# Late sums of the down weights on VectorE, an addition moved up, and rows of x loaded one by one, in a one-core hybrid encoder layer

## The chip, the cores and the metric

The kernel runs on one core of one Trainium2 chip. The metric is the device time of that core in microseconds (us), from the first to the last instruction with what the launch adds around it; three runs are given and their median is the time. Five engines work in parallel, each through its own list of instructions in order: TensorE (PE; its weight loads are shown apart as PEld), VectorE (DVE), ScalarE (ACT), GpSimd (POOL) and SyncE (SP), which here does nothing but issue transfers. An instruction waits until the results that it needs have been signalled by other engines or by transfers. An engine whose next instruction waits does nothing else meanwhile.

## The reference

One layer of an encoder on 2048 prompt tokens and 64 sample tokens, all in float32. The first half is a pooled mixer and an mLSTM with an output projection; the second half, which this change touches, is a gated feed-forward network with a causal convolution of four taps over the tokens:

```python
h2 = rmsnorm(x, g2) * (1 + sc2) + sh2
up = h2 @ w_up
upp = jnp.concatenate([conv_buf.astype(up.dtype), up], 1)
conv = b_conv + sum(w_conv[j] * upp[:, j:j + T] for j in range(CONV_W))
a, g = jnp.split(conv, 2, -1)
x = x + gt2 * ((jax.nn.silu(g) * a) @ w_down)
...
y_prompt = rmsnorm(xp, g_final)
```

The outputs are y for both sequences and the states of the mixer, the mLSTM and the convolution.

## The kernel before, in words

All products of matrices are done in three passes over float32 numbers split into a high and a low part (high by high, high by low, low by high), so each weight tile that comes in (`raw`) is turned into a split tile (`wt`): ScalarE makes the high part (L385), VectorE the low part (L388).

The feed-forward network runs from about 805 us on, in three groups of 704 tokens (`fgroups`, group 0, 1, 2), each of two half-rows of 352. The 22 blocks of 128 inner channels are taken in parts: (0,5), (5,10), (10,16), (16,22) in groups 0 and 1, and (0,6), (6,10), (10,14), (14,18), (18,22) in group 2. In each part the up products of its blocks are made, and then the down product adds them to the sum for the eight rows of 128 output channels. A down product of group 2 also saves multiplications (`quad_down`, L1785 on): it takes quads of 2x2 weight blocks and needs, beside two of the blocks themselves, four sums of blocks, which are kept in device memory as `dsum`.

A block of the up product is a `Pair` (the a-half and the g-half of the gate). Its four products of half-rows are made from seven products of 12 matmuls each, in the manner of Strassen and Winograd, from sums of the inputs and sums of the weights: in order B11, B21, the old pair's T4, T2, T3, B22, T1 (L1570 on; the matmuls are those of L1547). Their results are put together on VectorE: `eg` and `ea` are the two channels' convolution inputs (L1555, and L1609 for half of `ea`, which is the result of B21 plus a copy of B11's), `ta` and `tg` the taps (L1535, with a scaling on ScalarE, L1530), then the silu on ScalarE (L1656), the gate (L1663, or L1703 where the result goes into quads), and the split of the gated rows into `av` (L1682 on ScalarE, L1692 on VectorE). `ea` reads the PSUM bank of B21; B22 writes into this bank next. The steps of two older pairs are woven into the products of the newest one.

Work of the stages that lie before or after is kept in six lists of generators (`bg[0]` to `bg[5]`); `tick(i)` runs list i one step further, up to its next `yield`. List 0 holds the final normalization of the group before (`final`: the updates of x at L1893 and the stores of y), list 1 the preparation of the next group (normalization, then `reload`, which fetches the next group's inputs), list 5 the sums of the down weights (`down_sums`, L1771). In the last part of group 2, `from_quads` (L1829) turns the Strassen sums back into rows and adds them to x: per couple of rows two additions (L1838, L1839) and four updates (L1843); x itself is loaded per row by `load_x2` (L1862).

The order on TensorE, VectorE, ScalarE and GpSimd is the order in which the program is written (`manual_schedule`); the transfers that SyncE issues are placed by a scheduler, except those that are marked to keep the order of the program. The weights come through SyncE's queue in the order of their use.

`down_sums` before: in 4 passes over column blocks, for each of the four sums, 4 transfers copy one summand to `dsum` through SyncE's queue (L1778), then 4 transfers issued by GpSimd (L1781) add the other summand on the way. Those are 64 copies and 64 adding transfers of 128 KB, spread over groups 0 and 1 (three ticks per pair).

## Time and profile before

| what | value |
|---|---|
| three runs | 2208.61, 2206.72, 2208.37 us; median 2208.37 |
| profiled execution | 2210.41 us, span 2208.6 us, granted clock 0.998 |
| TensorE, weight loads | busy 2176.4 us (99%), 2064.1 us (93%) |
| VectorE, ScalarE, GpSimd | 1626.1 us (74%), 1037.4 us (47%), 276.9 us (13%) |
| transfers | 521.68 MB, 236 GB/s on the mean |
| the feed-forward groups | about 804 to 1272, 1272 to 1740, 1740 to 2209 us |
| adding transfers of `dsum` (L1781) | 64 issues of 897 ns, from 825.9 to 1673.2 us |

A row of the groups reads: line, engine, operation, output <- input, shape, count, then busy time and mean ns of one, then the idle time of the engine just before the group and what ended it. A row of the timeline reads: start, length, engine, line, operation, names, count, and in brackets the idle time before it with its releaser. PEld rows show the weight loads that go ahead of each matmul. A row of the windows reads: the window, its length, the busy time of PE, PEld, DVE, ACT and POOL with their instructions, the granted clock, the share of the DMA engines and GB/s.

### The profile page before, as it was taken

How to read it: one execution, taken by the hardware profiler on the slowest of the kernel's cores; microseconds unless marked ns; L12 is line 12 of the kernel's file. 1: busy time of each engine (PE TensorE's matmuls, PEld its weight loads, DVE VectorE, ACT ScalarE, POOL GpSimd, SP SyncE). 2: the span in 40 equal slices, each digit the busy share in tenths (PEclk: the TensorE clock that was granted, in tenths of full speed). 3: DMA queues.
4: the chain of work that ended last, by engine and by line, in shares of the span. 5: the costliest groups of instructions: out<-in, count | busy, mean ns of one | idle time of the engine just before them, and what ended most of it. 6: DMA issues, size and time to landing. Idle time of an engine off the chain costs nothing. (4 is left out here: it accounts for less than half of the span.)

```text
span 2208.6 us, 38414 instructions
## 1 busy us (share of the span) xinstructions
PE 2176.4 (99%) x13708; PEld 2064.1 (93%) x13708; DVE 1626.1 (74%) x2996; ACT 1037.4 (47%) x2023; POOL 276.9 (13%) x546
## 2 busy tenths in 40 slices
PE   8999999999999999999999999999999999999998
PEld 7888888888899999999999999999999999999998
DVE  4887659577765768786958677776757597888894
ACT  3653335234243446464626444545435356554554
POOL 0010001001000101010202220101101321121122
PEclk9999999999999999999999999999999999999999
DMA  9978987997898687677858977767569665555552
GB/s 345 358 249 258 333 282 236 326 322 245 291 324 270 214 298 239 224 232 239 236 166 239 308 234 222 222 213 204 176 180 270 194 200 174 162 156 178 156 195 81
DMA packets 304192, 521.68 MB, mean 236 GB/s; under 512 B 27480, under 2 KB 131288, under 8 KB 304000
## 3 DMA queue, kind: packets, MB, share of 16 engines
q1 hardware_dynamic: 283008, 482.74, 66.8%
q10 hardware_dynamic: 11776, 28.09, 3.4%
q0 software_dynamic: 9216, 8.39, 3.1%
q8 instruction: 108, 1.77, 0.3%
q14 instruction: 84, 0.69, 0.1%
HBM read 408.36 MB, written 127.52 MB: 243 GB/s over the span
## 5 line engine op out<-in xcount | busy, mean ns | idle before, releaser
L1547 PE MATMUL mm<-hx,wt 128*128 128x352 f32 x5544 | 889.6, 321 | 10.0 <-DVE ea L1609 8.0
L1547 PEld LDWEIGHTS mm<-hx,wt 128*128 128x128 f32 x5544 | 879.5, 188 | 15.0 <-ACT wt L385 9.4
L442 PE MATMUL mm<-hl,wt 128*128 128x512 f32 (+2 forms) x1920 | 395.8, 358 | 1.4 <-DMA wt<-hl_kept 1.3
L2043 PE MATMUL mm<-av,wt 128*128 128x352 f32 (+2 forms) x2400 | 385.6, 321 | 1.6 <-ACT av L1682 0.9
L385 ACT ACTIVATE wt<-raw 128x512 fp32r<-128x512 f32 (+3 forms) x510 | 288.7, 579 | 205.5 <-PE mm L2043 64.6
L2043 PEld LDWEIGHTS mm<-av,wt 128*128 128x128 f32 x2400 | 380.7, 188 | 3.9 <-ACT av L1682 1.2
L388 DVE TENSOR_TENSOR wt<-raw,wt 128x512 fp32r<-128x512 f32 (+3 forms) x510 | 323.3, 648 | 73.6 <-ACT wt L385 71.3
L442 PEld LDWEIGHTS mm<-hl,wt 128*128 128x128 f32 x1920 | 312.7, 188 | 49.0 <-issue 2.8
L442 PE MATMUL mm<-mx,wt 128*128 128x512 f32 (+1 forms) x960 | 187.0, 354 | 0.3
L442 PEld LDWEIGHTS mm<-mx,wt 128*128 128x128 f32 x960 | 158.8, 188 | 25.8 <-ACT mx L1403 1.1
L385 ACT ACTIVATE wt<-wt 128x512 fp32r<-128x512 f32 x176 | 110.4, 628 | 123.8 <-DMA wt<-wsum 105.3
L388 DVE TENSOR_TENSOR wt<-wt 128x512 fp32r<-128x512 f32 x176 | 122.2, 694 | 58.9 <-ACT wt L385 58.5
L1535 DVE SCALAR_TENSOR_TENSOR tg<-eg,V,tg 128x704 f32<-128x704 f32 (+1 forms) x132 | 125.7, 952 | 40.9 <-ACT tg L1530 38.4
L2060 DVE SCALAR_TENSOR_TENSOR x<-mm,MOD,x 128x352 f32<-128x352 f32 (+4 forms) x152 | 78.0, 560 | 82.6 <-PE mm L2043 82.6
L1535 DVE SCALAR_TENSOR_TENSOR ta<-ea,V,ta 128x704 f32<-128x704 f32 (+1 forms) x132 | 125.7, 953 | 8.5 <-ACT ta L1530 5.9
L1796 PE MATMUL mm<-av,wt 128*128 128x352 f32 x576 | 94.4, 321 | 0.0
L1796 PEld LDWEIGHTS mm<-av,wt 128*128 128x128 f32 x576 | 91.8, 188 | 0.0
L207 DVE SCALAR_TENSOR_TENSOR acc<-raw,CA,acc 128x512 f32<-128x512 f32 x84 | 60.6, 748 | 30.8 <-DMA raw<-w_ada 30.7
L1656 ACT ACTIVATE tg<-tg 128x704 f32<-128x704 f32 (+1 forms) x66 | 52.3, 793 | 62.6 <-DVE tg L1535 62.6
L1555 DVE TENSOR_TENSOR eg<-mm,u 128x352 f32<-128x352 f32 x154 | 70.2, 468 | 14.8 <-ACT u L1625 10.1
L1605 ACT ACTIVATE u<-mm 128x352 f32<-128x352 f32 x66 | 30.3, 459 | 100.7 <-PE mm L1547 66.8
L1139 PE MATMUL mm<-wt,hl 128*128 128x256 f32 (+1 forms) x576 | 70.9, 282 | 0.0
(327 smaller groups left out, 2296.9 us busy)
## 6 DMA issues: line engine op xcount, KB each, us to landing
wt<-hl_kept SPq DMA_DIRECT2D x108, 512.0 KB, 5.9
raw<-w_up SPq DMA_DIRECT2D x198, 256.0 KB, 3.9
wt<-wsum SPq DMA_DIRECT2D x176, 256.0 KB, 4.8
wt<-wsplit SPq DMA_DIRECT2D x88, 512.0 KB, 4.8
w<-w_up SPq DMA_DIRECT2D x88, 256.0 KB, 5.4
wsum<-w SPq DMA_DIRECT2D x44, 512.0 KB, 6.2
wsplit<-wt SPq DMA_DIRECT2D x44, 512.0 KB, 4.4
raw<-w_down SPq DMA_DIRECT2D x88, 256.0 KB, 3.9
```

The costliest lines, as they stand in the source:

```text
L207: dve.scalar_tensor_tensor(out=acc[s], in0=w, scalar=CA[:, k, s:s + 1], in1=acc[s], op0=ALU.mult, op1=ALU.add)
L385: act.activation(u.w[:, 0, :u.n], u.raw[:, :u.n], AF.Copy)
L388: dve.tensor_tensor(out=u.w[:, 1, :u.n], in0=u.raw[:, :u.n], in1=u.w[:, 0, :u.n].bitcast(F32), op=ALU.subtract)
L442: pe.matmul(ps[bi][:, :hi - lo], U[:, a, k % 4 * P:(k % 4 + 1) * P], mv[k][:, b, lo:hi], start=(at == 0 and pi == 0), stop=(k == order[-1] ...
L1139: pe.matmul(ps[ti][:n, :cols], h[4 * kh + k4][:, b, lo:lo + n], U[:, a, k4 % 2 * cols:(k4 % 2 + 1) * cols], start=(kh == 0 and k4 == 0 and ...
L1535: dve.scalar_tensor_tensor(out=t[:, :E], in0=ext[:, j:j + E], scalar=wc(j, f), in1=t[:, :E], op0=ALU.mult, op1=ALU.add)
L1547: pe.matmul(ps[:, :FH], U[:, a, kc * P:(kc + 1) * P], Bo.at(nm, kc, b), start=(first and kc == 0 and pi == 0), stop=(kc == 3 and pi == 2), ...
L1555: dve.tensor_tensor(out=ext[:, d:d + b - a], in0=ps[:, a:b], in1=u[:, a:b], op=ALU.add)
L1656: act.activation(self.tg[:, :E], self.tg[:, :E], AF.Silu)
L1796: pe.matmul(ps, U[:, x, w:w + P], quad.d[nm][z], start=(start and k == 0 and pi == 0), stop=(k == 1 and pi == 2), skip_group_check=not start)
L2043: pe.matmul(ps[i][:, :hi - lo], U[:, a, k % 4 * P:(k % 4 + 1) * P], av[k](b, lo, hi), start=(k == 0 and (a, b) == PASSES[0]), stop=(k == n ...
L2060: dve.scalar_tensor_tensor(out=x3[n][:, a:b], in0=ps[i][:, a - lo:b - lo], scalar=gt2(n, s), in1=x3[n][:, a:b], op0=ALU.mult, op1=ALU.add)
```

## The change

1. `down_sums` is written anew. It enters list 5 at the third part of group 1 (part index 2) and first waits until list 1 is empty. Then it goes through 32 tiles: SyncE loads a tile of 2 KB per partition (one quad of blocks) from `w_quad`, which is laid out anew for this, into one of three tiles in rotation (`dq`, `rb`, `rbn`); VectorE makes the four sums in place by four additions of 128x128; GpSimd issues one store of the whole tile to `dsum`. List 5 is ticked once after each product (seven times per pair) and at every second step of a down product, and is emptied before group 2 begins. `dsum` has another layout, and `quad_units` and `quad_down` index it accordingly.
2. `ea` (now L1603) is added right after the taps of the old pair (L1534), ahead of `eg` and the weight split.
3. The rows of x in the first part of a group are loaded one at a time, each ahead of a row of the down product (`row(n)`), instead of all that are missing at once.
4. `final` of group 1 takes six ticks instead of three per row. `from_quads` has four steps per pair instead of six beside the last pairs, and what is left goes on list 1 in the last down product.
5. A small Silu on ScalarE is written ahead of the groups.

The order on TensorE is the same before and after but for names. Three places show what moves.

VectorE, a pair in the fourth part of group 1 (channels 16 to 21; `ta`, `tg` are the taps of the a- and the g-half, `wt<-wt` the low part of a summed weight, `wt<-raw,wt` that of a weight as loaded). Before:

```order
L388 TENSOR_TENSOR wt<-wt 128x512
L1535 SCALAR_TENSOR_TENSOR ta<-ea,V,ta 128x704 x2
L1555 TENSOR_TENSOR eg<-mm,u_18018 128x352
L388 TENSOR_TENSOR wt<-wt 128x512
L1609 TENSOR_TENSOR ea<-mm,s_18104 128x352
L1535 SCALAR_TENSOR_TENSOR tg<-eg,V,tg 128x704 x2
L388 TENSOR_TENSOR wt<-raw,wt 128x512 x2
```

Now:

```order
L1534 SCALAR_TENSOR_TENSOR ta<-ea,V,ta 128x704 x2
L1603 TENSOR_TENSOR ea<-mm,s_18089 128x352
L1555 TENSOR_TENSOR eg<-mm,u_17994 128x352
L387 TENSOR_TENSOR wt<-wt 128x512
L1786 TENSOR_TENSOR rb<-rb 128x128
L1787 TENSOR_TENSOR rb<-rb 128x128
L1788 TENSOR_TENSOR rb<-rb 128x128
L1789 TENSOR_TENSOR rb<-rb 128x128
L1534 SCALAR_TENSOR_TENSOR tg<-eg,V,tg 128x704 x2
L387 TENSOR_TENSOR wt<-raw,wt 128x512 x2
```

The addition of `ea` stands ahead of `eg` and of the weight split instead of behind them, and the four additions of a tile of the new sums stand between the split and the taps of the g-half. Such fours stand at three or four places of each pair of this part.

SyncE's queue in the same part (`wsum` and `wsplit` are sums of the up weights, `w_up` the weights themselves). Before:

```order
L369 DMA raw<-w_up 128x512 x3
L374 DMA wt<-wsplit 128x1024
L369 DMA raw<-w_up 128x512
L1778 DMA dsum<-dsum 128x256
L369 DMA raw<-w_up 128x512
L377 DMA wt<-wsum 128x512
L369 DMA raw<-w_up 128x512
L377 DMA wt<-wsum 128x512
L374 DMA wt<-wsplit 128x1024 x2
L377 DMA wt<-wsum 128x512
L1778 DMA dsum<-dsum 128x256
```

Now:

```order
L368 DMA raw<-w_up 128x512
L376 DMA wt<-wsum 128x512
L1780 DMA dq<-w_quad 128x512
L373 DMA wt<-wsplit 128x1024
L1780 DMA rbn<-w_quad 128x512
L373 DMA wt<-wsplit 128x1024
L1780 DMA rb<-w_quad 128x512
L376 DMA wt<-wsum 128x512
L1780 DMA rbn<-w_quad 128x512
L368 DMA raw<-w_up 128x512 x2
L376 DMA wt<-wsum 128x512
```

One copy in `dsum` every few rows has become a load of a whole tile about every second row, among the weights of the up products; each waits until the store of its tile's former content has landed.

SyncE's queue at the first down product of group 1. Before:

```order
L369 DMA raw<-w_up 128x512
L369 DMA raw<-w_down 128x512 x2
L369 DMA raw<-w_down 128x128 x2
L1778 DMA dsum<-dsum 128x256
L1862 DMA x_14581<-x2d 128x704
L1862 DMA x_14740<-x2d 128x704 x2
L1862 DMA x_14743<-x2d 128x704 x2
L369 DMA raw<-w_down 128x128
```

Now:

```order
L368 DMA raw<-w_up 128x512
L368 DMA raw<-w_down 128x512 x2
L368 DMA raw<-w_down 128x128 x2
L1871 DMA x_14504<-x2d 128x704
L1871 DMA x_14660<-x2d 128x704 x2
L368 DMA raw<-w_down 128x128
L368 DMA raw<-w_down 128x512
```

Ahead of the w_down rows stand three rows of x instead of a copy in `dsum` and five rows of x; the last two follow after the last rows of w_down, among the w_up weights of the next part.

The small Silu stands at the start of ScalarE's list, in the first stage. The diff, without the line that names the old sums:

```diff
--- before.py
+++ after.py
...
@@ -311,13 +310,13 @@
         kept = wsplit[f, KEPT.index(i)]
         return (kept, 512, WHOLE, None) if g else (wsum[f, :, i], 512, INSIDE, kept)
 
-    dsum = dr.tile([4, P, 4, NP * P], F32, tag="dsum", name="dsum")
+    dsum = dr.tile([4, P, NP, 2, 2 * P], F32, tag="dsum", name="dsum")
 
     def quad_units(m, j):
 
-        c = slice(j * 256, j * 256 + 256)
-        return [(w_down[2 * m, :, j * 512:(j + 1) * 512], 512), (dsum[m][:, S3D:S1D + 1, c], 512),
-                (dsum[m][:, S2D:S4D + 1, c], 512), (w_quad[3, m, :, c], 256)]
+        k = slice(2 * j, 2 * j + 2)
+        return [(w_down[2 * m, :, j * 512:(j + 1) * 512], 512), (dsum[m][:, k, 1], 512), (dsum[m][:, k, 0], 512),
+                (w_quad[m, :, k, 3], 256)]
 
     for g in range(NFG):
         for si, (f0, f1_) in enumerate(SPARTS if g in SGS else PARTS):
...
@@ -1548,6 +1547,7 @@
                           start=(first and kc == 0 and pi == 0), stop=(kc == 3 and pi == 2), skip_group_check=not first)
             if kc % 2:
                 tick(0)
+        tick(5)
         live[0] -= 1
 
     def plus(o, half, ext, u, ps):
...
@@ -1593,20 +1593,20 @@
             act.activation(self.s1, b1[:, :FH], AF.Copy)
             rest((older, Pair.split_hi))
             product(b2, Bo, "B21", True)
-            tick(5)
             rest((old, Pair.scale_a), (older, Pair.split_lo))
             extra(1)
             if old:
                 old.last_product()
-            rest((old, Pair.taps_a), (old, Pair.sum_g0))
+            rest((old, Pair.taps_a))
+            self.ea = ext_tile(o, f, "a")
+            for (a, b, d) in spans(o, 0):
+                dve.tensor_tensor(out=self.ea[:, d:d + b - a], in0=b2[:, a:b], in1=self.s1[:, a:b], op=ALU.add)
+            rest((old, Pair.sum_g0))
             extra(2)
             product(b1, Bo, "T2", False)
             self.u2 = half_tile("u2")
             act.activation(self.u2, b1[:, :FH], AF.Copy)
             rest((old, Pair.scale_g))
-            self.ea = ext_tile(o, f, "a")
-            for (a, b, d) in spans(o, 0):
-                dve.tensor_tensor(out=self.ea[:, d:d + b - a], in0=b2[:, a:b], in1=self.s1[:, a:b], op=ALU.add)
             self.b3 = mm_ps()
             extra(3)
             product(self.b3, Bo, "T3", True)
...
@@ -1616,9 +1616,7 @@
             product(self.b4, Bo, "B22", True)
             rest((old, Pair.silu))
             extra(5)
-            tick(5)
             product(b1, Bo, "T1", False)
-            tick(5)
 
         def copy_u4(self):
             self.u4 = half_tile("u4")
...
@@ -1770,16 +1768,27 @@
 
     def down_sums():
 
-        for j in range(NP // 2):
-            c = slice(j * 256, j * 256 + 256)
-            for s, start, more in ((S1D, 2, 3), (S3D, 0, 2), (S2D, S1D, 0), (S4D, S2D, 1)):
-                for m in range(4):
-                    src = w_quad[start, m, :, c] if s < S2D else dsum[m][:, start, c]
-                    tc.keep_in_program_order(nc.sync.dma_start(out=dsum[m][:, s, c], in_=src))
-                    yield
-                for m in range(4):
-                    pool.dma_start(out=dsum[m][:, s, c], in_=w_quad[more, m, :, c], accum_op=ALU.add)
-                    yield
+        while bg[1]:
+            yield
+        todo = [(j, m) for j in range(NP) for m in range(4)]
+        q = []
+        for i in range(len(todo) + 1):
+            if i < len(todo):
+                j, m = todo[i]
+                t = f1.tile([P, 4 * P], F32, tag="dq", name="dq") if i % 3 == 0 else fscr(("rb", "rbn")[i % 3 - 1])[:, :4 * P]
+                q.append(t)
+                tc.keep_in_program_order(nc.sync.dma_start(out=t, in_=w_quad[m, :, j].rearrange("p i c -> p (i c)")))
+            yield
+            if i:
+                j, m = todo[i - 1]
+                t = q[i - 1]
+                a11, a12, a21, a22 = (t[:, x * P:(x + 1) * P] for x in range(4))
+                dve.tensor_tensor(out=a22, in0=a21, in1=a22, op=ALU.add)
+                dve.tensor_tensor(out=a21, in0=a11, in1=a21, op=ALU.add)
+                dve.tensor_tensor(out=a11, in0=a22, in1=a11, op=ALU.add)
+                dve.tensor_tensor(out=a12, in0=a11, in1=a12, op=ALU.add)
+                pool.dma_start(out=dsum[m][:, j], in_=t.rearrange("p (a c) -> p a c", a=2))
+            yield
 
     def quad_down(o, j, two, Y, first, midway):
 
...
@@ -1791,7 +1800,7 @@
             def product(ps, u, i, nm, start, on=False):
                 U = W.at(u)
                 for k, quad in enumerate(two):
-                    w = (2 * k + i) * P if u == 0 else k * P if u == 3 else (2 * i + k) * P
+                    w = k * P if u == 3 else (2 * k + i) * P
                     for pi, (x, z) in enumerate(PASSES):
                         pe.matmul(ps, U[:, x, w:w + P], quad.d[nm][z], start=(start and k == 0 and pi == 0),
                                   stop=(k == 1 and pi == 2), skip_group_check=not start)
...
@@ -1894,7 +1903,7 @@
                                          in1=box[0][:, a:b], op0=ALU.mult, op1=ALU.mult)
                 yield
             act.dma_start(out=yT[k, :, o.t0:o.t0 + FT], in_=x3[k])
-            for _ in range(3):
+            for _ in range(6 if o.g + 1 in SGS else 3):
                 yield
 
     def final_end(o, x3, sums, lo, hi):
...
@@ -1955,13 +1964,17 @@
     ET = mybir.EngineType
     fctx.enter_context(tc.manual_schedule(engines={ET.PE, ET.Activation, ET.DVE, ET.Pool}))
     x3, ssum = [], None
-    bg[5].append(down_sums())
+    act.activation(RF[:, 0:1], V[:, 0:1], AF.Silu)
     for o in fgroups:
+        if o.g in SGS:
+            drain(5)
         Bo = B[o.g]
         quads, more, held = {}, [], []
         Y = None
         for pi, (f0, f1_) in enumerate(SPARTS if o.g in SGS else PARTS):
             lastp = f1_ == NF
+            if o.g + 1 in SGS and pi == 2:
+                bg[5].append(down_sums())
             if o.g in SGS and lastp:
                 av = [None] * (NF - PARTS[-1][0])
             nf = f1_ - (PARTS[-1][0] if o.g in SGS and lastp else f0)
...
@@ -1975,7 +1988,7 @@
                 if lastp:
                     made = []
                     conv = from_quads(o, Y, x3, made)
-                    turn_back = [(i, lambda: next(conv, None)) for i in range(6)]
+                    turn_back = [(i, lambda: next(conv, None)) for i in range(4)]
                     more = [[(0, was.taps_a), (0, lambda: lo.append(q.plain(0, av))), (1, was.taps_g), (1, was.silu),
                              (1, lambda: lo[0]()), (2, was.gate), (3, lambda: lo.append(q.plain(1, av))),
                              (4, lambda: lo[1]()), (5, lambda: next(conv))]] + [turn_back] * 3
...
@@ -2025,8 +2038,9 @@
                 do(9)
                 held.append(pair)
                 continue
-            if pi == 0 and o.g > 0:
-                x3 += load_x2(o, range(len(x3), KD))
+            def row(n):
+                if len(x3) <= n < KD:
+                    x3.extend(load_x2(o, range(len(x3), n + 1)))
             if not o.last:
                 if lastp:
                     drain(0, 1)
...
@@ -2034,6 +2048,8 @@
                     bg[1].append(reload(B[-1]))
             if lastp:
                 ssum = fscr("ssum")
+                if Y:
+                    bg[1].append(conv)
 
             def down(ps, W, ks, secs, stays=False):
                 for k in ks:
...
@@ -2047,8 +2063,10 @@
                     pump()
                     if todo:
                         do()
+                    elif o.last:
+                        tick(1 - k % 2)
                     else:
-                        tick(1 - k % 2)
+                        tick((1, 5)[k % 2])
 
             def down_end(n, ps, secs):
                 while Y and n not in made:
...
@@ -2080,6 +2098,7 @@
             todo.extend([both_of(pair.sum_g1, old.gate), both_of(pair.sum_a, old.split_hi), both_of(old.split_lo, pair.scale_a)])
             for n in range(NE - 1):
                 pss.append([mm_ps() for _ in both])
+                row(n)
                 down(pss[n], Ws[n], range(nf - 2), both)
                 if n == 0:
                     do(9)
...
@@ -2089,7 +2108,9 @@
             for n in range(NE - 1):
                 down(pss[n], Ws[n], [nf - 2], both)
             pss.append([mm_ps() for _ in both])
+            row(NE - 1)
             down(pss[-1], Ws[-1], range(nf - 1), both)
+            row(NE)
             do(9)
             for n in range(NE):
                 down(pss[n], Ws[n], [nf - 1], both)
...
@@ -2099,6 +2120,7 @@
                 sums = [(ssum, 0)]
                 for n in range(NE, KD):
                     ps = [mm_ps() for _ in secs]
+                    row(n + 1)
                     down(ps, rows[n], range(nf), secs, ends)
                     down_end(n, ps, secs)
                 if ends:
...
@@ -2166,7 +2188,7 @@
         "w_up": blocks(i["w_up"][0], KD),
         "w_down": blocks(i["w_down"][0], NF),
         "w_quad": blocks(i["w_down"][0], NF)[:, :, :2 * NP * P].reshape(4, 2, P, NP, 2, P).transpose(
-            1, 4, 0, 2, 3, 5).reshape(4, 4, P, NP * P),
+            0, 2, 3, 1, 4, 5).reshape(4, P, NP, 4, P),
         "st_C": np.concatenate([i["state_mlstm_C"][0, 0].transpose(2, 0, 1),
                                 i["state_mlstm_n"][0, 0].T[:, :, None]], 2),
         "st_pool": np.pad(i["state_pool"][0, 0].T.reshape(4, P, 15).transpose(1, 0, 2), ((0, 0), (0, 0), (1, 0))),
```

1 line of the change is left out of this document (removed).

## The prediction

> **What bounds the kernel now.** I read the page's busy shares first, then its costliest groups.
>
> ```profile
> PE 2176.4 (99%) x13708; PEld 2064.1 (93%) x13708; DVE 1626.1 (74%) x2996; ACT 1037.4 (47%) x2023; POOL 276.9 (13%) x546
> ...
> L1547 PE MATMUL mm<-hx,wt 128*128 128x352 f32 x5544 | 889.6, 321 | 10.0 <-DVE ea L1609 8.0
> ```
>
> TensorE is busy 99% of the span and its order of instructions is the same before and after. So the change can only win the small holes in TensorE's row, and lose whatever new holes it makes. The largest group, the up products, stood idle 10.0 us, 8.0 of it behind one VectorE addition, `ea` at L1609: the addition that moves. The waits of TensorE, and its timeline at some of them, say where:
>
> ```profile
> PE mm L1547 <- DVE ea L1609: 8.0, 10, 1.3
> ```
>
> ```profile
> 1026.26 26.86 PE L1547 MATMUL mm<-hx,wt 128*128 128x352 f32 x168 [0.98 <-DVE ea L1609]
> ...
> 1309.51 26.94 PE L1547 MATMUL mm<-hx,wt 128*128 128x352 f32 x168 [0.88 <-DVE ea L1609]
> ...
> 1355.13 0.59 PE L2043 MATMUL mm<-av,wt 128*128 128x352 f32 x2 [0.91 <-ACT av L1682]
> 1356.06 26.59 PE L2043 MATMUL mm<-av,wt 128*128 128x352 f32 x166 [0.34 <-DVE av L1692]
> ...
> 1549.59 17.51 PE L1547 MATMUL mm<-hx,wt 128*128 128x352 f32 x108 [0.28 <-DVE ea L1609]
> ```
>
> Ten waits, 8.0 us, the longest 1.3. The ends of matmuls are modelled, so the weight loads give the lost time better; they run 1 to 1 with the matmuls. Two of the same stalls there:
>
> ```profile
> 1309.47 0.19 PEld L1547 LDWEIGHTS mm<-hx,wt 128*128 128x128 f32 x1 [1.14 <-ACT wt L385]
> ```
>
> ```profile
> 1549.56 0.19 PEld L1547 LDWEIGHTS mm<-hx,wt 128*128 128x128 f32 x1 [0.55 <-ACT u L1605]
> ```
>
> 1.14 against 0.88 and 0.55 against 0.28: 0.26 more each, so the ten stalls cost about 8.0 + 10 × 0.26 = 10.6 us. That is the most the moved addition can give.
>
> **The moved addition.** The product B22 writes into the bank that `ea` reads, so its first matmul waits for `ea`; its third needs VectorE's weight split (L388). Before, VectorE ran taps, `eg`, split, `ea`; now taps, `ea`, `eg`, split. The work ahead of the split grows by `ea`'s 0.52 us, so the split now ends where `ea` ended. What is recovered depends on what stood between. Three kinds, as VectorE's timeline has them:
>
> ```profile
> 1304.96 1.94 DVE L1535 SCALAR_TENSOR_TENSOR ta<-ea,V,ta 128x704 f32<-128x704 f32 x2
> 1306.81 0.52 DVE L1555 TENSOR_TENSOR eg<-mm,u 128x352 f32<-128x352 f32 x1
> 1307.25 0.68 DVE L388 TENSOR_TENSOR wt<-wt 128x512 fp32r<-128x512 f32 x1
> 1307.85 1.08 DVE L1893 SCALAR_TENSOR_TENSOR x<-x,V,rb 128x352 f32<-128x352 f32 x2
> 1308.84 0.52 DVE L1609 TENSOR_TENSOR ea<-mm,s 128x352 f32<-128x352 f32 x1
> ```
>
> Here two updates of x (1.08 us) stood ahead of `ea`. TensorE was ready at 1309.47 − 1.14 = 1308.33. Now `ea` ends near 1307.3 and the split near 1308.4, and the third matmul is due at 1308.65 (two matmuls at 0.16: 85 in 13.30 us, below). The whole 1.14 comes back. The stall at 1791 has the same form; I take 0.84.
>
> ```profile
> 1547.89 0.52 DVE L1555 TENSOR_TENSOR eg<-mm,u 128x352 f32<-128x352 f32 x1
> 1548.32 0.68 DVE L388 TENSOR_TENSOR wt<-wt 128x512 fp32r<-128x512 f32 x1
> 1548.92 0.52 DVE L1609 TENSOR_TENSOR ea<-mm,s 128x352 f32<-128x352 f32 x1
> ```
>
> Here nothing stood between. The split ends where `ea` did, so only the two matmuls that need no split slip into the hole: 0.32 us. Four stalls are of this kind (1054, 1549, 2100, 2142): 1.3 us.
>
> ```profile
> 1936.21 0.96 DVE L1703 TENSOR_TENSOR fscr<-ta,tg 128x640 f32<-128x640 f32 x2 [0.86 <-ACT tg L1656]
> ...
> 1937.52 0.69 DVE L388 TENSOR_TENSOR wt<-wt 128x512 fp32r<-128x512 f32 x1
> 1938.13 0.52 DVE L1609 TENSOR_TENSOR ea<-mm,s 128x352 f32<-128x352 f32 x1
> ```
>
> In the first pair of a part VectorE has a hole ahead of the split (0.86 us here), and `ea` now falls into it. At 1938 and 2019 I take 0.77 each, at 1026 and 1495 0.8 each: 3.1 us. Sum of the ten: 1.14 + 0.84 + 1.3 + 3.1 = 6.4 us. Bounds: 10 × 0.32 = 3.2 and 10.6.
>
> **Rows of x one by one.** The stall of 0.91 and 0.34 us at 1355 above is the end of a chain that starts in SyncE's queue:
>
> ```profile
> 1340.35 0.48 SPq L1778 DMA_DIRECT2D dsum<-dsum  x1
> 1340.89 2.48 SPq L1862 DMA_DIRECT2D x<-x2d  x5
> ```
>
> ```profile
> 1349.29 0.31 ACT L385 ACTIVATE wt<-raw 128x128 fp32r<-128x128 f32 x1 [3.52 <-DMA raw<-w_down]
> ...
> 1354.29 0.79 ACT L1682 ACTIVATE av<-tg 128x704 fp32r<-128x704 f32 x1 [0.44 <-DVE tg L1663]
> ```
>
> Six transfers stand ahead of the w_down rows; ScalarE waits 3.52 us for the rows, and taps, silu, gate and `av` behind them come late. Now three rows of x stand there and no `dsum`. That is 3 of 6 issues and about half the bytes, so the rows should land 2 to 3 us sooner. TensorE loses 0.91 + 0.34 plus 2 × 0.26, 1.8 us; I take all of it, bounds 0 and 1.8. Rows 6 and 7 are loaded later, before the down product that adds to them; nothing waits there.
>
> **Turning the sums back.** In the last group two thirds of this work ran beside the pairs where VectorE is full:
>
> ```profile
> 2110.00:2120.00 10.00, 10.00 (x65) 10.00 (x64) 9.38 (x18) 4.73 (x9) 1.06 (x4) 1.00 0.70 241
> 2120.00:2130.00 10.00, 9.54 (x61) 9.28 (x60) 9.93 (x20) 4.93 (x9) 3.87 (x6) 1.00 0.83 272
> 2130.00:2140.00 10.00, 10.00 (x64) 9.73 (x63) 9.96 (x21) 4.92 (x9) 5.19 (x6) 1.00 0.63 209
> ```
>
> (Length, then PE, PEld, DVE, ACT and POOL busy.) The weight loads lose 0.72 + 0.27 us in the last two windows. Two steps fewer per pair take the fourth couple of rows, some 3 us of VectorE (two additions of 0.52 and four updates), into the last down product, where VectorE waits for TensorE. I take 1.0 us, bounds 0 and 2.2 (these 0.99 and the part of the stall at 2142, the longest of the ten, that the moved addition leaves).
>
> **The new sums.** The 64 adding transfers and 64 copies go; 32 tiles of 256 KB come, each a load, four VectorE additions of 128x128 and a store that GpSimd issues. They begin only in the third part of group 1. About 5 run in the down product before 1614, 20 beside the pairs from 1614 to 1692, 7 in the last down product. The pairs before:
>
> ```profile
> 1640.90:1654.20 13.30, 13.30 (x86) 13.30 (x85) 10.29 (x16) 7.30 (x12) 0.98 (x4) 1.00 0.68 205
> ...
> sum 77.86, PE 77.86 PEld 77.86 DVE 54.90 ACT 39.05 POOL 9.86; mean PE 12.98 PEld 12.98 DVE 9.15 ACT 6.51 POOL 1.64
> ```
>
> ```profile
> L388 DVE TENSOR_TENSOR wt<-raw,wt 128x512 fp32r<-128x512 f32 (+3 forms) x510 | 323.3, 648 | 73.6 <-ACT wt L385 71.3
> ...
> L388 DVE TENSOR_TENSOR wt<-raw,wt 128x128 fp32r<-128x128 f32 x32 | 9.0, 286 | 0.0
> ```
>
> An addition of that size takes 0.286 us, and two of the four wait for the one before. Four make 1.1 to 1.2 us. VectorE is busy 54.90 of 77.86 us; 20 tiles add 22 to 24, so it is full (77 to 79). Some of that falls into holes that are there:
>
> ```profile
> 1642.48 0.89 DVE L1692 TENSOR_TENSOR av<-tg,av 128x704 fp32r<-128x704 f32 x1 [1.57 <-ACT av L1682]
> ...
> 1648.41 1.94 DVE L1535 SCALAR_TENSOR_TENSOR tg<-eg,V,tg 128x704 f32<-128x704 f32 x2 [1.07 <-ACT tg L1530]
> ```
>
> Two tiles a pair fit these; a pair of 13.3 us (seven products of 1.9) has room in the order for 3.3 tiles, so the other 1.3 push the weight splits back, and TensorE waits once their lead is used up. The nearest rows are those of 2110 to 2140: VectorE 98% busy, weight loads short by 0.99 of 30 us, 3.3%, which on 77.86 us is 2.6. I take 3 us. Bounds: 0 if the splits' lead absorbs all; 12 if some ten tiles that meet no hole cost their whole 1.2.
>
> The removed transfers were off TensorE's path; I give them 0. The early Silu on ScalarE lands in the start phase, where ScalarE is not the bound: 0, and if it costs, its own third of a microsecond.
>
> **Sum.** The profiled execution took 2210.41 us, span 2208.6. −6.4 − 1.8 − 1.0 + 3 = −6.2, so 2204.2 for it. It stands 2.0 us above the median of the runs, 2208.37; that median becomes 2202.2.
>
> **Rivals.** (a) The wait only changes its name. Every B22 then waits for the split at L388 and each stall gives 0.32 us: −3.2 − 1.8 − 1.0 + 3 = −3.0, 2205.4. For it: four of the ten have this form. Against it: the rows of 1309 and 1938, where something else stood in the way.
>
> (b) VectorE's fullness eats the gain. The 1.3 tiles per pair that meet no hole cost their whole 1.2 us in about five pairs, 8 us: −6.4 − 1.8 − 1.0 + 8 = −1.2, 2207.2. For it: 77 to 79 us of work in 77.86. Against it: the 3.3% of the windows from 2110 to 2140.
>
> (c) Slower: the ring of three tiles holds the weights. A tile's next load waits for its store, in SyncE's queue, with the weights of the up products queued behind it, and VectorE's splits are queued behind additions that wait for the load. Times to landing before:
>
> ```profile
> raw<-w_up SPq DMA_DIRECT2D x198, 256.0 KB, 3.9
> wt<-wsum SPq DMA_DIRECT2D x176, 256.0 KB, 4.8
> ...
> dsum<-w_quad POOLq DMA_DIRECT2D x64, 128.0 KB, 4.7
> ```
>
> Load 4.8, additions 1.2, issue 0.8, store 4.7: 11.5 us. The ring turns every 6 products, 6 × 1.9 = 11.4 us. With 1 us more in each of the two transfers (20 tiles bring 10.5 MB more into the stretch) a turn takes 13.5, 2.1 too long in each of 20/3 turns: 14 us in place of 3. −9.2 + 14 = +4.8, so 2213.2. From 12.8 us per turn on (1.4 × 20/3 = 9.2) the gain is gone. Against it: the DMA share in the pair shown was 0.68, not full.
>
> A page speaks for (c). The Trainium skill, SBUF — State Buffer, section "SBUF: two separate sides", says that VectorE and GpSimd share a port pair under an exclusive lock, and that a transfer issued by GpSimd waits for its descriptors while VectorE holds it. By it the stores behind the additions would be issued late. No row of such a store exists before; GpSimd's issues in this stretch look unhindered:
>
> ```profile
> 1632.63 1.65 POOL L1781 DMA_DIRECT2D dsum<-w_quad  x2 [0.42 <-issue]
> ```
>
> 0.82 each, in a stretch where VectorE was 70% busy. The trace does not bear it out, so far as it reaches; the lock adds nothing to (c)'s chance.
>
> **How the numbers follow.** Forecast 0.52, (a) 0.15, (b) 0.14, (c) 0.19. The range reaches from the gains at the better end (−8.5 − 1.8 − 1.5 + 0, 2196.5) to (c) a little under its price, 2212; the forecast's own is 2197 to 2205. A measurement of this kernel tells about 0.2% (4.4 us) from no change. Forecast and part of (a), (b) lie beyond that: faster 0.56; same 0.27; slower 0.17.
>
> **What would show it.** Right: no `ea` among TensorE's waits; no stall at 1355; 13.3 us per pair between 1600 and 1690 with VectorE near 10 of 10. Wrong: TensorE waiting for L388 with VectorE waiting for a `w_quad` load before it (c), holes of over 1 us in every pair of that stretch (b), or ten stalls of 0.8 now laid to L388 (a).

## The result, and the profile after

The changed kernel takes 2216.94 us (median of 5 runs, 2214.0 to 2220.18), the kernel before, timed beside it, 2206.72 (2204.68 to 2208.61): ratio 1.0046, 95% interval 1.0031 to 1.0062. It is slower by some 10 us, where 6 us less were forecast. The profiled execution took 2214.0, its span is 2212.2 us. All ratios in this document are of fast executions; one of 10869.2 us of the kernel before and one of 2674.34 us of the kernel with all tiles at half the pace are not in them.

TensorE's rows start the stages, so the stage lengths can be read from the first row of each in the two timelines. In us:

| stage | before | after |
|---|---|---|
| first up product at | 804.6 | 800.3 |
| group 0 | 467.6 | 462.0 |
| group 1 up to its last part | 342.3 | 341.3 |
| the six pairs of the last part | 77.9 | 88.3 |
| last down product of group 1 | 47.6 | 51.9 |
| group 2 to the end | 468.6 | 468.4 |

The loss is where the new sums are. The other stages are level or shorter. The 4.3 us ahead of the first up product can't be laid to the change: in the four kernels whose sums and first half are the old ones (before, and the three parts tried alone below) that row stands at 800.2 to 804.9. The waits of TensorE after:

```profile
...
PE mm L1546 <- ACT s L1593: 2.4, 2, 1.6
...
PE mm L1546 <- ACT wt L384: 2.1, 1, 2.1
PE mm L1546 <- DVE eg L1555: 2.1, 4, 0.9
PE mm L1546 <- DVE wt L387: 2.1, 7, 0.4
PE mm L2059 <- DVE wt L387: 1.9, 1, 1.9
```

The ten waits on `ea` are gone. In their place stand a few long ones, and TensorE's timeline after puts most of them into the last part of group 1 and behind it:

```profile
1626.87 6.24 PE L1546 MATMUL mm<-hx,wt 128*128 128x352 f32 x26 [2.14 <-ACT wt L384]
...
1651.92 6.30 PE L1546 MATMUL mm<-hx,wt 128*128 128x352 f32 x38 [0.89 <-DVE eg L1555]
...
1681.53 10.50 PE L1546 MATMUL mm<-hx,wt 128*128 128x352 f32 x60 [0.87 <-DVE eg L1555]
...
1694.56 5.01 PE L2059 MATMUL mm<-av,wt 128*128 128x352 f32 x20 [1.90 <-DVE wt L387]
...
1749.33 1.23 PE L1546 MATMUL mm<-hx,wt 128*128 128x352 f32 x6 [1.60 <-ACT s L1593]
```

The longest one, 2.14 us, can be followed back. SyncE's timeline after:

```profile
1609.60 0.33 SPq L1780 DMA_DIRECT2D rb<-w_quad  x1
1611.39 0.33 SPq L376 DMA_DIRECT2D wt<-wsum  x1
1617.34 0.33 SPq L1780 DMA_DIRECT2D rbn<-w_quad  x1
1617.78 1.23 SPq L368 DMA_DIRECT2D raw<-w_up  x2
1619.10 0.38 SPq L376 DMA_DIRECT2D wt<-wsum  x1
```

and VectorE's and ScalarE's:

```profile
1612.83 0.29 DVE L1786 TENSOR_TENSOR rbn<-rbn 128x128 f32<-128x128 f32 x1 [4.01 <-DMA rbn<-w_quad]
```

```profile
1626.18 0.63 ACT L384 ACTIVATE wt<-wt 128x512 fp32r<-128x512 f32 x1 [6.05 <-DMA wt<-wsum]
```

VectorE waited 4.01 us for tile `rbn`, so its store went out late; the next load into `rbn` waited at the head of SyncE's queue until 1617.34, nearly 6 us with nothing issued; three weight loads stood behind it. Then all went out at once, `wt<-wsum` at 1619.10 landed 7 us later, ScalarE split it at 1626.18, and TensorE stood. The waits of SyncE give the sum, 60.0 us in 20 waits for stores of the ring:

```profile
SPq L1780 <- DMA dsum<-rbn: 24.4, 7, 5.5
SPq L1780 <- DMA dsum<-rb: 23.2, 9, 5.8
...
SPq L1780 <- DMA dsum<-dq: 12.4, 4, 4.5
```

### The profile page after: what moved, and what is told of

The parts are those of the page before. It is cut to its first block, busy times and chain, and to the rows that moved or that the text cites. A ratio compares the mean times of both kernels' runs of the same rounds, so it can differ in the third digit from the quotient of the medians.

```text
span 2212.2 us, 38389 instructions
## 1 busy us (share of the span) xinstructions
PE 2182.5 (99%) x13708; PEld 2069.5 (94%) x13708; DVE 1663.5 (75%) x3124; ACT 1038.2 (47%) x2024; POOL 230.1 (10%) x514
## 3 DMA queue, kind: packets, MB, share of 16 engines
q8 instruction: 108, 1.77, 0.3%
## 5 line engine op out<-in xcount | busy, mean ns | idle before, releaser
L1534 DVE SCALAR_TENSOR_TENSOR tg<-eg,V,tg 128x704 f32<-128x704 f32 (+1 forms) x132 | 125.7, 952 | 30.6 <-ACT tg L1529 28.2
L387 DVE TENSOR_TENSOR wt<-wt 128x512 fp32r<-128x512 f32 x176 | 119.2, 686 | 30.3 <-ACT wt L384 30.1
L1534 DVE SCALAR_TENSOR_TENSOR ta<-ea,V,ta 128x704 f32<-128x704 f32 (+1 forms) x132 | 125.6, 951 | 7.1 <-ACT ta L1529 4.8
```

Source lines behind the costliest of these rows:

```text
L387: dve.tensor_tensor(out=u.w[:, 1, :u.n], in0=u.raw[:, :u.n], in1=u.w[:, 0, :u.n].bitcast(F32), op=ALU.subtract)
L1534: dve.scalar_tensor_tensor(out=t[:, :E], in0=ext[:, j:j + E], scalar=wc(j, f), in1=t[:, :E], op0=ALU.mult, op1=ALU.add)
```

## The experiments

Two theories stood after this: the **ring** of three tiles turns too slowly and holds whatever queue waits for it; or VectorE is **full**, and each tile's 1.2 us of additions delays the pairs. A third: some other part of the change costs. The kernel before was timed beside every batch (medians 2204.57 to 2204.77).

### Everything but the sums

```diff
  kernel before
+ ea moved up; row(n); six ticks in final; four steps of turning back, conv on list 1; Silu
  (down_sums, dsum and its ticks unchanged)
```

> The kernel before with everything of the change but the sums: the addition of ea moved up, rows of x one by one, six ticks in the final, four steps of turning back, the Silu. The sums stay as they were (64 copies and 64 adding transfers over groups 0 and 1). Both theories (the ring of three tiles holds SyncE's queue; VectorE has no room for the additions) put the whole loss on the new sums, so this kernel must show the forecast gain of the rest: 6 to 10 us under the kernel before, ratio 0.9955 to 0.9975, no TensorE wait on ea, 40 us instead of 41.8 for the first down product of group 1. If a part of the rest is what loses (a third theory), it is slower than before.

Measured: 2198.5 us, ratio 0.9973 (0.9962 to 0.9984). Stages: group 0 465.3, then 340.5, 77.9, 47.6, 464.7. Of TensorE's long waits in the feed-forward groups little is left:

```profile
PE mm L1547 <- DVE wt L388: 2.1, 6, 0.4
```

So the loss is in the sums, and the rest gains about 6 us. This kernel beats both. Stage by stage the changed kernel stands to it at −3.3 (group 0), +0.8, +10.3, +4.3 and +3.7 us.

### The ring without additions

```diff
- dve.tensor_tensor(out=a22, in0=a21, in1=a22, op=ALU.add)   (and the three behind it)
```

> The changed kernel without the four VectorE additions per tile: tiles are loaded and stored unsummed, so the down weights' sums are left out (the output of the last group is not the reference's). Loads, stores, the ring of three and the order of the queues stay. Theory ring: SyncE still waits some 40 to 60 us for stores in that stretch, TensorE still loses 8 us or more between 1603 and 1700, time 2210 or above. Theory full VectorE: the stretch of six pairs is back at 78 to 80 us, time 2198 to 2203.

Measured: 2214.2 us, ratio 1.0043 (1.0028 to 1.0057). The six pairs take 85.7 us, VectorE is busy only 55.30 of them; SyncE waits 44.2 us for stores:

```profile
1605.45:1691.11 85.66, 82.07 (x495) 80.49 (x493) 55.30 (x82) 38.50 (x66) 16.52 (x43) 0.96 0.81 283
```

```profile
SPq L1780 <- DMA dsum<-dq: 17.0, 4, 5.8
...
SPq L1780 <- DMA dsum<-rbn: 13.8, 4, 5.5
SPq L1780 <- DMA dsum<-rb: 13.4, 3, 5.8
```

With no addition at all nearly the whole loss stays, 7.7 us of it in the pairs and more at the start of group 2, whose first weights SyncE issues late (TensorE waits 3.63 us there for `s`). The ring is enough to cause a loss of that size. Its turns in the pairs take 12.5 us in the mean, against the 11.4 us that six products give it.

### The additions without the ring

```diff
  kernel of "everything but the sums", with a list 6 ticked where the new list 5 is
+ t = f1.tile([P, 4 * P], F32, tag="dq"); pool.memset(t, 0.0)
+ ...
+ for i in range(33):
+     yield
+     if i: (the four additions in place on t)
+     yield
```

> The kernel of e1_old_sums with the 128 additions put at the ticks at which the changed kernel has them, on a tile that stays in place (zeros), without loads and stores: VectorE's load of the changed kernel, no ring. The real sums come as in the kernel before. Theory full VectorE: the six pairs take 84 to 88 us, time about 2210 to 2216. Theory ring: the pairs take at most 81 us, time 2200 to 2205.

Measured: 2204.17 us, ratio 0.9995 (0.9986 to 1.0004), 5.7 us over the kernel of the first experiment. The pairs take 81.2 us, 3.3 more than without additions. From the second pair on:

```profile
1620.66:1688.62 67.96, 66.06 (x411) 64.61 (x410) 64.04 (x135) 34.64 (x58) 10.66 (x26) 1.00 0.71 215
```

VectorE is busy 64.04 of 67.96 us, 94%, and the weight loads fall short by 3.35. The full VectorE is real, and costs in the pairs about what the forecast put on it. It is the smaller part. The rest of the 5.7 us lies mostly in group 2 (467.3 us against 464.7), where no addition of this list is left. TensorE shows no wait for it there: in the first down product of that group 183 matmuls keep it busy for 30.1 us, 28.8 in the first experiment. The cause stays open.

### Loads by GpSimd

```diff
- tc.keep_in_program_order(nc.sync.dma_start(out=t, in_=w_quad[m, :, j]...))
+ pool.dma_start(out=t, in_=w_quad[m, :, j]...)
```

> The changed kernel with the 32 loads of tiles issued by GpSimd instead of SyncE: the same additions, stores, ring and bytes, but no load stands in SyncE's queue any more, so no weight waits behind a store. Theory of the held queue: the six pairs come down from 88 us to 80 to 83 (the additions alone took 81.2), the start of group 2 loses its stall, total 2203 to 2207. If it is the bytes or VectorE waiting for its tiles, the pairs stay at 85 or more and the total at 2211 or above.

Measured: 2214.68 us, ratio 1.0044 (1.0029 to 1.0058); the pairs take 93.2 us. My expectation of the held queue fell; its other branch, VectorE waiting for its tiles, is what came. SyncE's queue is free, but the ring is as slow as before (13.7 us per turn in the pairs), and now VectorE meets it, 21.8 us in 12 waits:

```profile
DVE rb L1786 <- DMA rb<-w_quad: 7.9, 4, 3.2
...
DVE rbn L1786 <- DMA rbn<-w_quad: 7.3, 4, 4.5
DVE dq L1786 <- DMA dq<-w_quad: 6.6, 4, 2.7
```

So it is not SyncE's queue in particular. Whichever queue in fixed order holds a wait for the ring passes it on to what stands behind it: SyncE by loading weights late, VectorE by doing its own work late. TensorE's two longest waits in these pairs (3.0 and 2.9 us) are for `ea`.

### One tile, spread from group 0 on

```diff
- 32 tiles in a ring of three, two ticks each, from part 2 of group 1 on
+ one tile dq: load, four ticks, additions and store, five ticks, next load; from group 0 on
```

> The changed kernel with the same 32 tiles, one tile in place of a ring of three, from the start of group 0 on, without waiting for list 1: load, four ticks later the additions and the store, five ticks later the next load (9 ticks of 1.9 us per tile; additions 1.18 us in 17 us). Both theories: the density was the loss, so it is gone: 6 to 10 us under the kernel before, like e1_old_sums within 2 us. If additions anywhere in a pair stop TensorE, 32 holes of some 0.3 us would be seen in groups 0 and 1, 2205 to 2209.

Measured: 2211.06 us, ratio 1.0031 (1.0018 to 1.0045), above both expectations. The last six pairs take 77.9 us again, but group 0 takes 469.2 and the first stretch of group 1 345.2. SyncE still waits 13.6 us for stores of the tile, in 6 waits of up to 3.5. The additions now fall among the pairs that also carry the next group's preparation; nine waits of TensorE in these pairs, of 0.2 to 0.9 us, are for VectorE's `eg` or a weight split, and one of 1.84 us at 1389 is for ScalarE's `s`. So this run does not tell what the additions cost from what the chain of the one tile costs.

### One tile per pair, in a hole of VectorE

```diff
  one tile dq, ticked only after B21 (additions, store) and after B22 (next load), where the pair has an old one
```

> The changed kernel with the sums spread from group 0 on, one tile per pair, one buffer: the load 6 products ahead, the four additions right ahead of the split of av, where VectorE waits 1.57 us for ScalarE in the kernel before. If the place in the pair decides what an addition costs, nothing is lost: within 2 us of e1_old_sums (2198.5), unlike e4_spread, whose additions fell anywhere. If 1.18 us more in a pair costs TensorE time in any place, 18 pairs of groups 0 and 1 each lose 0.2 to 0.4 us: 2203 to 2207.

Measured: 2210.77 us, ratio 1.0026 (1.0015 to 1.0038): no better, and above both expectations. Group 0 469.7, then 347.2; against the first experiment 4.4 + 6.7 = 11.1 us for 32 tiles, 0.35 each. TensorE's timeline at one such pair, and VectorE's ahead of it:

```profile
1065.30 0.56 PE L1546 MATMUL mm<-hx,wt 128*128 128x352 f32 x2 [0.74 <-DVE ea L1604]
1066.23 17.54 PE L1546 MATMUL mm<-hx,wt 128*128 128x352 f32 x108 [0.37 <-DVE wt L387]
```

```profile
1059.90 0.29 DVE L1779 TENSOR_TENSOR dq<-dq 128x128 f32<-128x128 f32 x1 [1.10 <-DMA dq<-w_quad]
```

The hole of 1.57 us was read in the last part of group 1; in the parts before it the preparation of the next group works on VectorE too, and I take it that this fills the hole (not tried by itself). Here VectorE first waits 1.10 us for the tile itself, and the wait and the additions together push the taps, `ea` (0.74) and the split (0.37) back. Over the run VectorE waits 6.7 us for tiles, in 7 waits. So the 0.35 us per tile holds late loads too, and is not the price of the additions alone.

### Only in the down products

```diff
  one tile dq, ticked at every step of a down product only: load, five steps, additions and store, three steps
```

> The changed kernel with the 32 tiles worked off only in the down products of groups 0 and 1 (about four in each of the eight), one tile in place of the ring: load, five steps later the additions and the store, three steps later the next load. There VectorE was 58% busy in the kernel before (27.9 of 47.8 us). Theory: an addition costs TensorE time only where VectorE's work is what TensorE waits for next, which is in the pairs. Then nothing is lost, 2197 to 2201, as e1_old_sums, and clearly under e4_spread and e8_one_per_pair (2211). If any 32 tiles through SyncE's queue cost some 10 us, it is at 2207 or above.

Measured: 2236.16 us, ratio 1.0149 (1.0132 to 1.0165), the worst of all, against my expectation. VectorE has room there, but a turn of eight steps is about 7.6 us, and the chain of load, additions and store needs more (8.5 us: the median landings of this run, 3.2 and 3.7, and 1.6 from the first addition to the store's issue). SyncE and VectorE wait in turn:

```profile
SPq L1772 <- DMA dsum<-dq: 64.2, 28, 7.4
```

```profile
DVE dq L1776 <- DMA dq<-w_quad: 77.1, 24, 5.3
```

The weights of the next part are queued behind, and TensorE stands up to 4.71 us at the start of a part. It is the same mechanism in a sharper form: the time given to a turn was shorter than the chain.

### Half the tiles at half the pace

```diff
- todo = [(j, m) for j in range(NP) for m in range(4)]      two ticks per tile
+ todo = [(j, m) for j in range(NP) for m in range(2)]      four ticks per tile
```

> The changed kernel with half the tiles (16) through the ring, at half the pace: 12 products per turn of the ring instead of 6. The other half is copied unsummed to its place in group 0 (16 transfers of 256 KB within the memory), so half of the down weights' sums are left out and the last group's output is not the reference's. If a turn of the ring that takes longer than its ticks is what holds the queues, the loss in the six pairs vanishes but for some 1.7 us (half of what the additions alone cost): pairs 78 to 80 us, total 2199 to 2204. If every tile costs its part wherever it comes, half of the loss stays: pairs 83 us, total about 2208.

Measured: 2200.57 us, ratio 0.9988 (0.9977 to 1.0). The six pairs:

```profile
1608.72:1686.65 77.93, 77.93 (x494) 77.93 (x493) 64.42 (x121) 38.85 (x66) 10.77 (x29) 1.00 0.77 250
```

(The scheduler placed the unsummed copies in the first 180 us, not in group 0.) Not one hole, with tiles, loads and stores passing and the transfers at 0.77 of their time, as in the changed kernel (0.78). So transfers at that share of their time make no hole by themselves; the slower pace takes the holes away. It also halves the ring's bytes per microsecond, and the two are not told apart: to run without a hole at full pace the changed kernel's pairs would have needed about 0.88 (an estimate, 0.78 × 88.27 / 77.93). SyncE waits for stores 4.6 us at most in one go and 10.9 in all.

### All tiles at half the pace, in two places

```diff
- if o.g + 1 in SGS and pi == 2: bg[5].append(down_sums())
+ if not o.last and pi == 2: bg[5].append(down_sums((2 * o.g, 2 * o.g + 1)))     (four ticks per tile)
```

> The changed kernel with all 32 tiles through the ring of three at half the pace: 16 tiles from the third part of group 0 on (when list 1 is empty there), 16 from the third part of group 1 on, four ticks per tile instead of two, 12 products (22.8 us) per turn of the ring. All sums are made. If the pace of the ring was what made the change slower, both stretches run without a hole (pairs 78 us), group 0 takes 462 us as in the changed kernel (465 with the old sums) and group 2 465 us: 2195 to 2201, under e1_old_sums' 2198.5 or level with it, ratio 0.995 to 0.9985. If tiles cost their part at any pace, 2206 or above.

Measured: 2202.49 us, ratio 0.9984 (0.9974 to 0.9993): a little faster than before, and by the two ratios 14 us under the changed kernel with the same 32 tiles, ring, additions and stores. The pairs of group 1's last part are without a hole (77.93 us). Group 0 is not, against the expectation: 467.0 us. The pairs of its last part, which carry tiles, take 79.5 us instead of 77.9, and TensorE waits in the down product behind them (0.81 and 0.34). So half the pace is slow enough in one of the two places and not quite in the other. It does not beat the old sums (0.9973; the intervals overlap).

### The other parts, one by one

```diff
  kernel before
+ ea moved up                                   (e5)
+ row(n) in place of load_x2 of all rows        (e6)
+ six ticks in final, four steps of turning back, conv on list 1   (e10)
```

> The kernel before with the addition of ea moved up and nothing else. By the forecast's own term it gains 6.4 us (bounds 3.2 and 10.6): ratio about 0.997, the ten waits on ea gone, groups 0, 1 and 2 shorter by some 2, 2 and 3 us. If the wait only changes its name, 3.2 us and ten waits on the weight split.

> The kernel before with the rows of x loaded one by one and nothing else. By the forecast's term: 1.8 us less, the first down product of group 1 40.0 us instead of 41.8. If the two late rows collide with the rows that the preparation of the next group loads, a new stall of TensorE stands at the start of the second part of group 1 (behind ScalarE's copy s), and the gain is 0 or turns into a loss of 1 to 3 us.

> The kernel before with six ticks in the final of group 1 and four steps of turning back beside the last pairs, the rest on list 1, and nothing else. By the forecast's term 1.0 us less (bounds 0 and 2.2). Since ea alone (ratio 0.9993) and rows alone (0.9997) leave about 4 of e1_old_sums' 6 us unexplained, it may be as much as 4 us (0.998), if the parts add up; if they do not, it is within 0.1% of before.

Measured ratios: `ea` 0.9993 (0.9983 to 1.0003), rows 0.9997 (0.9988 to 1.0007), turning back 0.9993 (0.9984 to 1.0003). None is told from no change alone. Together they make −0.17%, the first experiment with all of them −0.27% (−0.16 to −0.38), which the intervals allow. The Silu was not tried alone.

## Why the prediction was wrong

**The step that failed is the sum's term for the new sums: "I take 3 us", with bounds 0 and 12.** It priced the additions and left the ring to rival (c), at a chance of 0.19. Of its two halves the additions were sized well: 3.3 us in the pairs in the run with additions alone. The ring was not. Against the kernel with the old sums the changed kernel loses 10.3 + 4.3 + 3.7 + 0.8 us and wins 3.3: with the removed transfers, which I gave 0, the term measured 15.8 us in place of 3, beyond its bound of 12.

**Rival (c) is what happened**, nearly at its numbers, but its turn was right by luck. It asked for a turn of 12.8 us to lose the gain and worked with 13.5. The loads of `dq` after:

```profile
1606.47 0.33 SPq L1780 DMA_DIRECT2D dq<-w_quad  x1
...
1620.58 0.44 SPq L1780 DMA_DIRECT2D dq<-w_quad  x1
...
1688.21 0.33 SPq L1780 DMA_DIRECT2D dq<-w_quad  x1
```

Six turns from 1606.47 to 1688.21 are 13.6 us each, against 11.4 of ticks. Its price, 2213.2, lies below the 2216.94; the stalls after the stretch (1694, 1749) were not in it. Rival (c) had got to 13.5 by 1 us more in each of the two transfers, and that is not what the trace shows: in the pairs the loads landed after 5.0 us in the median and the stores after 4.5, together the 9.5 (4.8 + 4.7) that it started from. The 17 whole turns of the three tiles in the pairs take 13.4 us in the mean: 6.7 us from a load's issue to its first addition, where the chain had 4.8, and 6.7 us from there to the next load, where it had the same 6.7 (1.2 + 0.8 + 4.7). So the step that the chain had too short is the one from the load to the additions. Some loads landed late, one of `dq` after 8.8 us. And additions whose load had landed stood behind other work in VectorE's list:

```profile
1634.77 0.38 SPq L1780 DMA_DIRECT2D dq<-w_quad  x1
```

```profile
1643.33 0.29 DVE L1786 TENSOR_TENSOR dq<-dq 128x128 f32<-128x128 f32 x1
```

This tile had landed after 5.0 us, at 1639.8; VectorE, whose row shows no wait, comes to it 3.6 us later. The ring without additions shows the same from the other side: by its medians a turn needs 4.5 + 0.5 + 4.6 = 9.6 us, and it takes 12.5. Each step also waits for its place in a queue of fixed order, and that time was in no term of the chain. The chain stood at 11.5 us against 11.4 given even without it, and I still called the case the less likely one. The argument "the DMA share was 0.68, not full" did not bear on it: with half the tiles the share was 0.77 and nothing stalled.

**The gains were over-sized by the one profile they were read from.** That execution took 2210.41 us; 19 later runs of the same kernel have a median of 2204.57. Part of the 6 us lies ahead of the feed-forward groups, where the first up product started at 804.6 (800.2, 800.8 and 804.9 with the three parts tried alone). Its ten waits on `ea` made 8.0 us; in the two later kernels that leave `ea` in its old place (rows alone, turning back alone) they make less:

```profile
PE mm L1547 <- DVE ea L1609: 5.5, 10, 1.3
```

```profile
PE mm L1547 <- DVE ea L1609: 5.1, 10, 0.9
```

So the term of 6.4 us was too large; `ea` alone measured −0.07%, 1.5 us (between 3.7 less and 0.7 more). Rival (a) was partly right too: with `ea` moved alone there are no waits on `ea`, and seven that carry the name of the split:

```profile
PE mm L1547 <- DVE wt L388: 3.8, 7, 1.2
```

Some 5.3 us of waits less these 3.8 leave 1.5, what was measured. The largest of them (1.18 us at 1783) is the stall at 1791, of which I had given back 0.84 as of the same form as the one at 1309. VectorE there, with `ea` moved:

```profile
1781.12 0.52 DVE L1555 TENSOR_TENSOR eg<-mm,u 128x352 f32<-128x352 f32 x1
1781.55 0.88 DVE L1732 TENSOR_TENSOR av<-fscr,av 128x704 fp32r<-128x704 f32 x1
1782.35 0.68 DVE L388 TENSOR_TENSOR wt<-wt 128x512 fp32r<-128x512 f32 x1
```

The split of `av` (0.88) stands between `eg` and the weight split, as it did before the change, so the weight split, not `ea`, ends last. The form was misread: at 1309 nothing stood there.

**Rows of x: the term was right, and was partly paid back.** The first down product of group 1 takes 39.93 us after against 41.76 (1.83 less; 1.8 were forecast). But rows 6 and 7, put later, stand in SyncE's queue among the rows that the preparation of the next group loads (`fscr<-x2d`): the second of these goes out 5.1 us ahead of the first product of the next part, where it went out 9.7 us ahead before. In the changed kernel:

```profile
1373.35 1.08 DVE L725 SCALAR_TENSOR_TENSOR fscr<-fscr,G,rbn 128x640 f32<-128x640 f32 x2 [4.44 <-DMA fscr<-x2d]
```

```profile
1374.27 1.07 ACT L727 ACTIVATE fscr<-fscr,MOD 128x640 f32<-128x640 f32 x2 [1.17 <-DVE fscr L725]
1375.24 0.44 ACT L1593 ACTIVATE s<-mm 128x352 f32<-128x352 f32 x1
```

and TensorE waits 0.82 us for `s` at 1375.73 (1.36 with the rows alone). In the kernel of the first experiment the load goes out as late, and `s` ends just in time. "Nothing waits there" was wrong.

**The removed transfers may not have been worth 0.** Group 0 takes 462.0 to 462.8 us in the four kernels that run neither the old transfers nor new tiles there, 464.2 to 465.5 in the three that keep the old ones with `ea` moved: 2 to 3 us. That is one profile of each, and the kernels that keep both the old transfers and `ea` in its place differ by more (463.6, 465.3 and 467.6), so it is not shown. **Turning back** fits its 1.0 us within what can be told (−0.07%).

**Rival (b)** holds for its sign, not its size: 3.3 us in the pairs, not 8.

The lock that the prediction cites from the Trainium skill (SBUF — State Buffer, section "SBUF: two separate sides") did not make the stores late: GpSimd's issues of the stores took 539 ns each in the median. There the Trainium skill tells of held transfers for VectorE in a 2-port mode; against a VectorE instruction with two SBUF inputs it names only a GpSimd one that reads SBUF, so the prediction applied the rule more widely than it is stated. The other way round the lock shows, below.

## What to carry to other kernels

For a ring of buffers whose steps sit in queues of fixed order, compare the whole turn (load, work, store, their landings) with the time the ring is given. Medians of the landings are not enough: add what late landings cost, and the time for which each step waits for its place in its queue (together some 2 to 3 us per turn here). When turn and time are about equal, take the stall as the forecast. A wait at the head of a queue costs everything that is queued behind it, and moving it to another queue only changes who passes it on; a slower pace removed it here, wholly in one of two stretches. A ring of more tiles was not tried. Gains read from the waits of one profile should be set against the spread of the runs: this one was 6 us above its kernel's median.

## What the hardware showed beyond that

**A TensorE hole of about 2 us can be followed by 3.4 us at half the granted clock.** After the stall that ends at 1626.87 the windows of the changed kernel show it (the clock is the third figure from the end):

```profile
1624.00:1626.00 2.00, 0.72 (x5) 0.43 (x3) 0.96 (x2) 0.00 (x0) 0.30 (x2) 1.00 0.99 373
1626.00:1628.00 2.00, 1.13 (x3) 0.71 (x4) 0.69 (x1) 1.81 (x4) 0.00 (x0) 0.79 0.87 333
1628.00:1630.00 2.00, 2.00 (x8) 2.00 (x8) 0.45 (x2) 1.06 (x3) 0.00 (x0) 0.50 0.78 304
```

Cut finer, the clock is 0.50 from 1627.2 to 1630.5 and 1.00 from 1630.6 on. 8 matmuls lie in the last of these windows, where 14 lie in 2 us at full clock (1636 to 1638). The same follows the stall of 1.90 us at 1694.56. So 3.4 us at half the clock cost about 1.5 us more, much of the price of the stall once again. The stalls of 0.9 us (1651.92, 1681.53) and of 1.60 us (1749.33) had no such window behind them, nor had the ten waits of the kernel before. The other runs narrow it: single holes of 1.84 us had such a window behind them (one tile spread, at 1389; only in the down products, at 1508), and single holes of 1.75 and 1.77 us had none (turning back alone, at 440; two halves at half the pace, at 438). But the length of one hole is not the whole rule: in the ring without additions a hole of 1.45 us at 1669.83, with another of 0.61 us 3 us behind it, lies by a window of 6.8 us, and holes of 2.9 to 4.7 us lie by windows of 3.4 to 10.2 us. By these rows a few long holes cost more than many short ones of the same sum.

**A GpSimd addition holds a VectorE instruction.** In the changed kernel, on the two engines:

```profile
1738.09 1.85 DVE L387 TENSOR_TENSOR wt<-raw,wt 128x512 fp32r<-128x512 f32 x1 [1.05 <-ACT wt L384]
```

```profile
1737.69 1.70 POOL L1962 TENSOR_TENSOR ssum<-ssum,fscr 128x704 f32<-128x704 f32 x1 [1.60 <-ACT fscr L1961]
```

A split that takes 0.69 us elsewhere took 1.85, and ended 0.55 us after GpSimd's addition did. It is not alone: of the 418 splits of this shape in the changed kernel six took over 1 us, and of those in the kernel before nine; each of the fifteen began while a GpSimd addition ran and ended 0.55 us after it. Additions of the new sums that met one took up to 1.74 in place of 0.29. This is what the Trainium skill states in SBUF — State Buffer, section "SBUF: two separate sides", of an exclusive lock for a VectorE instruction with two SBUF inputs against a GpSimd one that reads SBUF. It is read here from such pairs of rows, and was not tried by itself.
